# Thirty-two single zeros written into the output at the head, and the seventh pair's store cut in halves

## The chip, the cores and the metric

The kernel runs on one core of one Trainium2 chip. The metric is the device time in microseconds of one execution; the median of three runs is given. Traces come from one profiled execution, whose span runs from the first to the last instruction.

## The reference

A 3x3 convolution with padding 1 over 16 images of 64 channels and 64x64 points, to 128 output channels, in float32:

```python
x:      (16, 64, 64, 64) float32
weight: (128, 64, 3, 3) float32
x_pad = np.pad(x, ((0, 0), (0, 0), (1, 1), (1, 1)), mode='constant')
for b, co, ci, kh, kw:
    output[b, co] += weight[co, ci, kh, kw] * x_pad[b, ci, kh:kh+64, kw:kw+64]
```

The input has 16.8 MB and the output 33.6 MB.

## The kernel before

The images are worked on in eight pairs (`NP` = 8). The 64 channels of the first image of a pair lie in partitions 0 to 63, those of the second in 64 to 127, and TensorE multiplies each half by itself (`p0 = 64 * b2`).

The rows of an output image are taken two at a time. For an output row pair, the three vertical taps G0, G1, G2 are shared out: `U` is G1 times the sum of the two middle input rows (tile `ss`), `A` is (G2 - G1) and G0 on single rows, `Bt` is (G0 - G1) and G2 on single rows. The even output row is `A + U` and the odd one `Bt + U`, so 5 products of rows stand in for 6. `group` (L123) issues the matmuls of one such sum for 8 row pairs, three horizontal taps and both images, with float16 operands and float32 sums in PSUM.

At the head SyncE's queue issues the weights (`w_raw`, L42), the first pair `x0` (L45) and the pairs 1 to 3 (`xf`, L49), all in float32. VectorE sets `zeros` (L51). GpSimd casts the weights (L61); TensorE turns them (L93); ScalarE copies them to `Wt` (L94); GpSimd makes the two differences (L96, L97). Ten matmuls on `zeros` (`spin`, tile `warm`, L56) fill TensorE's time until the first pair is there. Pairs 4 to 7 are loaded by GpSimd's queue, which casts them to float16 on the way (`load`, L67, tile `xs`). For the pairs 0 to 3 ScalarE casts `x0` and `xf` to `xs` (L101, L169). The row sums `ss` are made on VectorE for pair 0 and on GpSimd for the others (L76).

The main loop (L111) runs over the pairs, and in a pair over four blocks of 8 row pairs. In each block ScalarE copies `U` from PSUM to `ut` (L164), and VectorE adds it to `A` (L174) and to `Bt` (L177) into the two output tiles `ot` of the pair. The first image of a pair is stored by SyncE's queue as soon as its last rows are added; the store of the second is put on a list, `held`, and ScalarE's queue issues it in the next block after the two `ut` copies (L171), or after the loop (L184). The helper `store` (L105) issues one DMA.

A table, `parts` (L178), says after which block which rows are stored. Pairs 0 to 6 are stored whole after the fourth block: one DMA of 2 MB for each image. Pair 7 is stored in two halves of 32 rows, after the second and the fourth block: two DMAs of 1 MB for each image.

Instructions under `keep` stay in program order on their engine. Tiles come from pools: `opool` has eight buffers of 16 KB in each partition, for `x0`, `xf` and `ot` alike. The DMAs issued by SyncE and ScalarE use eight completion semaphores in turn, so a store may have to wait for the DMA that was issued eight before it. Writes to the same image of the output are ordered by a wait on the earlier one's completion.

Of the kernel before, what the change touches and what calls it, by code (L numbers as in the profile page):

```python
# [8 lines left out]
F32 = mybir.dt.float32  # L9
# [4 lines left out]
def kernel(  # L14
# [6 lines left out]
    nc = tc.nc  # L21
    B, CI, H, W = x.shape
    CO = weight.shape[0]
    assert H == 64 and W == 64 and CI == 64 and CO == 128 and B % 2 == 0
    NP = B // 2
    RB = 8

    keep = tc.keep_in_program_order
    x_rows = x.rearrange("b c h w -> (b c) h w")
    out_rows = out.rearrange("b co h w -> b co h w")  # L30
    w_flat = weight.rearrange("co ci kh kw -> co (ci kh kw)")

    const = ctx.enter_context(tc.tile_pool(name="const", bufs=1))
# [15 lines left out]
        nc.sync.dma_start(xf[p], x_rows[128 * p : 128 * p + 128, :, :])  # L49
    zeros = const.tile([128, 512], F16)  # L50
    keep(nc.vector.memset(zeros, 0.0))  # L51
    warm = psum.tile([128, 512], F32, tag="acc", name="warm")

    def spin(n):
# [10 lines left out]
    def load(p):  # L65
        xs[p] = xpool.tile([128, H, W], F16, tag="xs", name="xs")
        keep(nc.gpsimd.dma_start(xs[p], x_rows[128 * p : 128 * p + 128, :, :]))  # L67
# [3 lines left out]
    def sums(eng, p, src, lo, n):  # L71
        if p not in ss:
            ss[p] = spool.tile([128, H // 2, W], F16, tag="ss", name="ss")
        v = src.rearrange("p (j i) c -> p j i c", i=2)
        keep(
            eng.tensor_add(  # L76
                ss[p][:, lo : lo + n, :], v[:, lo : lo + n, 0, :], v[:, lo : lo + n, 1, :]
            )
        )
# [25 lines left out]
    def store(eng, p, b2, ot, lo, hi):  # L105
        return eng.dma_start(
            out_rows[2 * p + b2, :, lo:hi, :],
            ot.rearrange("p j i c -> p (j i) c")[:, lo:hi, :],
        )

    for p in range(NP):  # L111
        if p + 1 < NP:
            for lo in (0, 16):
                sums(nc.gpsimd, p + 1, xf.get(p + 1, xs[p + 1]), lo, 16)
        if p > 0 and p + 4 < NP:
            load(p + 4)
        ots = [
            opool.tile([128, H // 2, 2, W], F32, tag="ot", name="ot") for _ in range(2)
        ]
        for blk in range(4):  # L120
            j0 = blk * RB

            def group(wi_rows):  # L123

                tiles = [
                    psum.tile([128, RB, W], F32, tag="acc", name="acc") for _ in range(2)
                ]
                n = 3 * len(wi_rows)
                i = 0
                for wi, off in wi_rows:  # L130
                    for kw in (1, 0, 2):
                        c_lo, c_hi = max(0, 1 - kw), min(W, W + 1 - kw)
                        for b2 in range(2):
                            p0 = 64 * b2
                            lo, hi = j0, j0 + RB
                            if off is None:
                                rhs = ss[p][p0 : p0 + 64, lo:hi, c_lo + kw - 1 : c_hi + kw - 1]
                            else:
                                while 2 * lo + off < 0:
                                    lo += 1  # L140
                                while 2 * (hi - 1) + off > H - 1:
                                    hi -= 1
                                first = 2 * lo + off
                                last = 2 * (hi - 1) + off
                                rhs = xs[p][
                                    p0 : p0 + 64,
                                    first : last + 1 : 2,
                                    c_lo + kw - 1 : c_hi + kw - 1,
                                ]
                            nc.tensor.matmul(  # L150
                                tiles[b2][:, lo - j0 : hi - j0, c_lo:c_hi],
                                Wt[p0 : p0 + 64, wi, kw, :],
                                rhs,
                                start=i == 0,
                                stop=i == n - 1,
                            )
                        i += 1
                return tiles

            U = group([(G1, None)])  # L160
            us = []
            for b2 in range(2):
                ut = upool.tile([128, RB, W], F32, tag="ut", name="ut")
                keep(nc.scalar.copy(ut, U[b2]))  # L164
                us.append(ut)
            if p + 1 in xf:
                q = p + 1
                for lo in {2: (0, 16), 3: (32, 48)}.get(blk, ()):
                    keep(nc.scalar.copy(xs[q][:, lo : lo + 16, :], xf[q][:, lo : lo + 16, :]))  # L169
            while held:  # L170
                keep(store(nc.scalar, *held.pop(0)))  # L171
            A = group([(G21, 1), (G0, -1)])
            for b2 in range(2):
                nc.vector.tensor_add(ots[b2][:, j0 : j0 + RB, 0, :], A[b2], us[b2])  # L174
            Bt = group([(G01, 0), (G2, 2)])
            for b2 in range(2):
                nc.vector.tensor_add(ots[b2][:, j0 : j0 + RB, 1, :], Bt[b2], us[b2])  # L177
            parts = {3: (0, 64)} if p < NP - 1 else {1: (0, 32), 3: (32, 64)}  # L178
            if blk in parts:
                lo, hi = parts[blk]  # L180
                store(nc.sync, p, 0, ots[0], lo, hi)
                held.append((p, 1, ots[1], lo, hi))
# [32 lines left out]
```

## Time and profile before

| | |
|---|---|
| Median of three runs | 126.49 us (126.47 to 126.51) |
| Profiled execution, span from first to last instruction | 124.78 us |
| Rest of an execution (median less the span) | 1.71 us |
| TensorE busy with the convolution (L150) | 9.9 to 112.5 us |
| Last store issued, landed | 113.95 us, 123.82 us |
| Bytes moved by DMA | 46.57 MB, mean 373 GB/s |
| Read from HBM, written to HBM | 17.07 MB, 33.55 MB |
| Store of 2 MB, issue to landing (median of seven, SyncE and ScalarE) | 22.0 and 18.9 us |
| Store of 1 MB, issue to landing (median of two) | 10.6 and 11.0 us |
| Granted TensorE clock over the span | 0.963 |

The time of the profiled execution itself is not listed beside its span; its span and the median are compared instead. The page counts the bytes of a DMA where they land, so that a load which turns float32 into float16 shows half of what it reads. The stage tables give, for a stretch of the span, each engine's busy time with its number of instructions, and in the last three columns the granted clock, the busy share of the 16 DMA engines and the GB/s. A packet is put to the stretch in which it starts, so a share can be a little over 1.

### The profile page before, as it was taken

To read this page: it belongs to the slowest core of one execution; us is meant where nothing else is said; L and a number is where in the kernel's file an instruction comes from. 1 tells how busy PE (TensorE), PEld (TensorE's weight loads), DVE (VectorE), ACT (ScalarE), POOL (GpSimd) and SP (SyncE) were. 2 spreads that over 40 slices of the span, in tenths; PEclk is the share of its full clock that TensorE was granted. 3 is DMA by queue.
4 is the path that set the end of the run, shared out by engine and by line. 5 is a ranking of instruction groups with operands and counts; after the bars stand their busy time and mean duration, and the time that the engine had idled before them with its cause. 6 is when DMAs were issued, how large, how long until landed. Compare 5 with 4: busy or idle time off the path is not lost.

```text
span 124.8 us, 2437 instructions
## 1 busy us (share of the span) xinstructions
PE 108.2 (87%) x988; PEld 49.3 (40%) x988; DVE 82.8 (66%) x133; ACT 52.0 (42%) x84; POOL 36.2 (29%) x27
## 2 busy tenths in 40 slices
PE   0699999999999999999999999999999999990000
PEld 0433444444444444444444444444444444440000
DVE  0016787878878787877777778777877787685000
ACT  4319749833993399333333333333333333330000
POOL 2360086294799202920067000940000000000000
PEclk9999999999999999999999999999999999999555
DMA  6899999999999999999999999999999999999991
GB/s 173 362 436 407 297 323 349 425 315 415 397 349 368 305 376 373 360 334 362 381 347 360 334 344 412 431 431 425 425 441 420 436 415 425 436 412 418 436 402 74
DMA packets 3898, 46.57 MB, mean 373 GB/s; under 512 B 432, under 2 KB 432, under 8 KB 560
## 3 DMA queue, kind: packets, MB, share of 16 engines
q1 hardware_dynamic: 2016, 25.46, 49.5%
q10 hardware_dynamic: 1296, 16.78, 31.6%
q0 software_dynamic: 576, 4.19, 16.1%
q8 instruction: 7, 0.11, 0.3%
q14 instruction: 3, 0.02, 0.0%
HBM read 17.07 MB, written 33.55 MB: 406 GB/s over the span
## 4 chain that ended last, share of the span: by engine, by line
PE 86%; DMA 2%; DVE 1%; issue 1%; POOL 1%; DVEq 0%
PE acc L150 81%; PE warm L56 4%; DMA w_raw<-in_weight_dram 2%; PE wp L93 1%; DVE ot L174 1%; POOL w L61 1%; DVE ot L177 0%; DVEq L210 0%; DVEq L174 0%
## 5 line engine op out<-in xcount | busy, mean ns | idle before, releaser
L150 PE MATMUL acc<-xs,Wt 64*128 64x504 f16 (+3 forms) x768 | 87.0, 373 | 0.0
L150 PEld LDWEIGHTS <-Wt 64*128 64x128 f16 x960 | 46.8, 94 | 56.2 <-issue 0.8
L164 ACT COPY ut<-acc 128x512 f32<-128x512 f32 x64 | 34.3, 588 | 52.9 <-issue 32.1
L174 DVE TENSOR_TENSOR ot<-acc,ut 128x512 f32<-128x512 f32 x64 | 41.2, 686 | 22.6 <-PE acc L150 18.3
L177 DVE TENSOR_TENSOR ot<-acc,ut 128x512 f32<-128x512 f32 x64 | 41.1, 684 | 0.0
L150 PE MATMUL acc<-ss,Wt 64*128 64x504 f16 (+1 forms) x192 | 26.0, 377 | 0.0
L76 POOL TENSOR_TENSOR ss<-xs 128x1024 f16<-128x1024 f16 x8 | 16.8, 2124 | 20.2 <-DMA xs<-in_x_dram 20.2
L76 POOL TENSOR_TENSOR ss<-xf 128x1024 f16<-128x1024 f32 x6 | 14.1, 2361 | 13.6 <-DMA xf<-in_x_dram 13.6
L169 ACT CAST xs<-xf 128x1024 f16<-128x1024 f32 x12 | 12.0, 1058 | 0.0
L76 DVE TENSOR_TENSOR ss<-x 128x512 f16<-128x512 f32 x4 | 2.5, 687 | 7.7 <-DMA x<-in_x_dram 7.7
L93 PE MATMUL wp<-ident,w 128*64 128x128 f16 x18 | 1.3, 328 | 4.3 <-POOL w L61 4.3
L101 ACT CAST xs<-x 128x1024 f16<-128x1024 f32 (+2 forms) x4 | 3.9, 1042 | 2.6 <-DMA x<-in_x_dram 2.6
L67 POOL DMA_DIRECT2D xs<-in_x_dram x4 | 2.4, 600 | 7.8 <-ACT xs L169 7.8
L56 PE MATMUL warm<-zeros 128*128 128x512 f16 x10 | 4.4, 631 | 0.0
L93 PEld LDWEIGHTS <-w 128*64 128x64 f16 x18 | 1.1, 210 | 4.3 <-POOL w L61 4.3
L94 ACT CAST Wt<-wp 128x384 f16<-128x384 f32 x3 | 1.2, 487 | 2.9 <-PE wp L93 2.9
L56 PEld LDWEIGHTS <-zeros 128*128 128x128 f16 x10 | 1.3, 143 | 2.3 <-issue 2.2
L94 ACT ACT_TABLE_LOAD x1 | 1.3, 1283 | 0.7 <-PEq L199 0.7
L96 POOL TENSOR_TENSOR Wt<-Wt 128x384 f16<-128x384 f16 x1 | 0.9, 907 | 1.7 <-ACT Wt L94 1.7
L61 POOL CAST w<-w_raw 128x576 f16<-128x576 f32 x1 | 0.7, 663 | 2.3 <-DMA w_raw<-in_weight_dram 2.3
L97 POOL TENSOR_TENSOR Wt<-Wt 128x384 f16<-128x384 f16 x1 | 0.9, 910 | 0.0
L51 DVE MEMSET zeros<- 128x256 uint32 x1 | 0.3, 272 | 0.9 <-PEq L199 0.9
(6 smaller groups left out, 0.9 us busy)
## 6 DMA issues: line engine op xcount, KB each, us to landing
out_dram<-ot SPq DMA_DIRECT2D x7, 2048.0 KB, 22.0
out_dram<-ot ACTq DMA_DIRECT2D x7, 2048.0 KB, 18.9
xf<-in_x_dram SPq DMA_DIRECT2D x3, 2048.0 KB, 22.1
xs<-in_x_dram POOLq DMA_DIRECT2D x4, 1024.0 KB, 23.4
x<-in_x_dram SPq DMA_DIRECT2D x1, 2048.0 KB, 7.6
out_dram<-ot SPq DMA_DIRECT2D x2, 1024.0 KB, 10.6
out_dram<-ot ACTq DMA_DIRECT2D x2, 1024.0 KB, 11.0
w_raw<-in_weight_dram SPq DMA_DIRECT2D x1, 288.0 KB, 2.8
```

The costliest lines, as they stand in the source:

```text
L56: keep(nc.tensor.matmul(warm, zeros[:, 0:128], zeros))
L61: keep(nc.gpsimd.tensor_copy(w16, w_raw))
L67: keep(nc.gpsimd.dma_start(xs[p], x_rows[128 * p : 128 * p + 128, :, :]))
L76: eng.tensor_add(ss[p][:, lo : lo + n, :], v[:, lo : lo + n, 0, :], v[:, lo : lo + n, 1, :])
L93: keep(nc.tensor.matmul(wp[q : q + 64, k * CO : k * CO + CO], w16[:, t::9], ident))
L94: keep(nc.scalar.copy(wrow(g), wp[:, 0 : 3 * CO]))
L101: keep(nc.scalar.copy(xs[0][:, lo:hi, :], x0[:, lo:hi, :]))
L150: nc.tensor.matmul(tiles[b2][:, lo - j0 : hi - j0, c_lo:c_hi], Wt[p0 : p0 + 64, wi, kw, :], rhs, start=i == 0, stop=i == n - 1,)
L164: keep(nc.scalar.copy(ut, U[b2]))
L169: keep(nc.scalar.copy(xs[q][:, lo : lo + 16, :], xf[q][:, lo : lo + 16, :]))
L174: nc.vector.tensor_add(ots[b2][:, j0 : j0 + RB, 0, :], A[b2], us[b2])
L177: nc.vector.tensor_add(ots[b2][:, j0 : j0 + RB, 1, :], Bt[b2], us[b2])
```

## The change

ScalarE first copies 32 zeros of type float32 into a tile of one element in each of 32 partitions, and its queue issues one DMA that writes them into the output: into the first point of every eighth channel of images 0 and 1. The first stores of these images write over them later, and wait for this DMA. The table `parts` now has the seventh pair (p = 6) stored in halves of 32 rows as well, like the eighth.

```diff
     zeros = const.tile([128, 512], F16)
     keep(nc.vector.memset(zeros, 0.0))
+    first = const.tile([32, 1], F32)
+    keep(nc.scalar.copy(first, zeros[0:32, 0:1]))
+    keep(
+        nc.scalar.dma_start(
+            out_rows[0:2, 0:CO:8, 0, 0:1].rearrange("b c w -> c b w"), first
+        )
+    )
     warm = psum.tile([128, 512], F32, tag="acc", name="warm")
...
-            parts = {3: (0, 64)} if p < NP - 1 else {1: (0, 32), 3: (32, 64)}
+            parts = {3: (0, 64)} if p < NP - 2 else {1: (0, 32), 3: (32, 64)}
```

In the changed program the order of the instructions on TensorE, VectorE and GpSimd is the same; ScalarE has the copy and the DMA between its table load and the first `Wt` cast, and ScalarE and SyncE each issue two stores of 1 MB for pair 6 in place of one of 2 MB.

## The prediction

> **What bounds the kernel now.** I read the page first (spans, slices, queues), then the stage table of engine and DMA time in short stretches, then the timeline around the first stores, then the packet records of the trace.
>
> ```profile
> span 124.8 us, 2437 instructions
> PE 108.2 (87%) x988; PEld 49.3 (40%) x988; DVE 82.8 (66%) x133; ACT 52.0 (42%) x84; POOL 36.2 (29%) x27
> ...
> DMA  6899999999999999999999999999999999999991
> ...
> q1 hardware_dynamic: 2016, 25.46, 49.5%
> q10 hardware_dynamic: 1296, 16.78, 31.6%
> q0 software_dynamic: 576, 4.19, 16.1%
> ```
>
> q1 is SP's queue, q10 ScalarE's, q0 GpSimd's; together their packets fill 97.2% of 16 engines' span. TensorE is busy without a break from 9.9 to 112.5 us, and the chain of waits runs through it, but the last store is issued at 113.95 us and lands at 123.82 us. The stage table says what fills those ten microseconds.
>
> ```profile
> 114.00:116.00 2.00, 0.00 (x0) 0.00 (x0) 0.00 (x0) 0.00 (x0) 0.00 (x0) 0.92 1.02 434
> 120.00:121.00 1.00, 0.00 (x0) 0.00 (x0) 0.00 (x0) 0.00 (x0) 0.00 (x0) 0.50 1.04 442
> 121.00:122.00 1.00, 0.00 (x0) 0.00 (x0) 0.00 (x0) 0.00 (x0) 0.00 (x0) 0.50 0.72 303
> 122.00:123.00 1.00, 0.00 (x0) 0.00 (x0) 0.00 (x0) 0.00 (x0) 0.00 (x0) 0.50 0.30 123
> ```
>
> The last three columns are granted clock, DMA share and GB/s. With every compute engine idle, the DMA engines still run full at about 430 GB/s until 121.2 us and then fall dry one by one. In the packet records there are 16 packets in flight from about 2 to 121.2 us. So the end is set by the sum of DMA work, about 9 us of which is still queued when TensorE stops. An earlier issue alone buys nothing; fewer engine-microseconds per packet do. The question is where the DMA engines are full but slow, and there is one place after the head:
>
> ```profile
> 24.00:25.00 1.00, 1.00 (x12) 0.49 (x10) 0.40 (x2) 0.70 (x2) 0.70 (x1) 1.00 1.01 426
> 25.00:26.00 1.00, 1.00 (x12) 0.49 (x10) 1.00 (x2) 0.00 (x0) 1.00 (x1) 1.00 1.25 459
> 26.00:27.00 1.00, 1.00 (x14) 0.41 (x10) 1.00 (x3) 0.20 (x1) 1.00 (x2) 1.00 1.17 279
> 27.00:28.00 1.00, 1.00 (x12) 0.47 (x10) 0.39 (x1) 0.87 (x2) 1.00 (x1) 1.00 0.71 213
> 28.00:29.00 1.00, 1.00 (x14) 0.47 (x10) 0.89 (x2) 0.00 (x0) 1.00 (x2) 1.00 0.77 328
> 29.00:30.00 1.00, 1.00 (x12) 0.42 (x10) 1.00 (x3) 0.00 (x0) 0.50 (x1) 1.00 1.03 442
> ```
>
> From 25 to 30 us the five rows carry 1721 KB where 5 x 430 = 2150 would go: 429 KB, or 1.0 us of all 16 engines, is lost. The packets say the same: reads of `xf` (16 KB, else 611 ns) take 800 to 1736 ns there, 0.94 us too long per engine, on all engines. The first two stores into the output were issued just before:
>
> ```profile
> 23.70 0.35 SPq L106 DMA_DIRECT2D out_dram<-ot  x1
> 24.30 0.38 ACTq L106 DMA_DIRECT2D out_dram<-ot  x1
> ```
>
> Their first packets start at 28.5 us and take 611 ns, nothing more. No later pair of stores shows such a dip (425 to 430 GB/s from 101 us on, where the seventh pair is issued). So something that happens once, with the first writes to the output, slows the reads beside it. The head has a smaller one of the same kind:
>
> ```profile
> 3.00:4.00 1.00, 0.00 (x0) 0.00 (x0) 0.00 (x0) 0.00 (x0) 0.41 (x1) 1.00 0.70 248
> 4.00:5.00 1.00, 0.69 (x12) 0.70 (x14) 0.00 (x0) 0.04 (x1) 0.25 (x1) 1.00 0.88 377
> 5.00:6.00 1.00, 1.00 (x14) 0.61 (x11) 0.00 (x0) 1.00 (x3) 0.09 (x1) 1.00 0.99 426
> ```
>
> There the first reads of the weights lose 0.26 us per engine (2304-byte packets, 93 ns as a rule, up to 498 ns at first) and the first reads of `x0` 0.41 us (up to 1506 ns).
>
> The sums below are made against the profiled execution: span 124.78 us from first to last instruction. The median of the runs is 126.49 us, so 1.71 us lies around the span; I take it as unchanged and add each difference to the median. One part in 500, 0.25 us, is about what a measurement of this kernel tells from no change.
>
> **The change, part by part.**
>
> *The zeros.* ScalarE's table load (0.74 to 2.02 us) stays first; the 32x1 copy waits for the memset (ends at 1.13 us), so it runs at about 2.05 us, and the DMA is issued at about 2.3 us. Issues on SP took 0.38 to 0.73 us, so ScalarE is free by about 3.1 us; what is queued behind it, the first `Wt` cast, starts at 4.96 us, when TensorE releases it. Cover 1.9 us, cost zero; if the cover were gone, ten `warm` matmuls (4.4 us) still stand between the casts and the first convolution matmul. The first stores of pair 0 now also wait for the zeros to land. These were issued 21 us before; the longest landing of a DMA issued at the head while others were ahead of it is 29.08 us, but that one was fourth in line on SP's queue, and ScalarE's queue is empty then. Behind that wait would stand ScalarE's `ut` copies, but I cost it at nothing.
>
> What the zeros cost the DMA engines: two packets of 4 bytes each, plus a semaphore packet. The trace has 4-byte packets only as semaphore writes (9 ns), so the floor is 3 x 9 = 27 ns per engine. The ceiling is the whole stall paid in the new place: 0.94 us. The nearest row for a small transfer that touches a new tensor is the weights' 0.26 us. I take that.
>
> What they save: if the stall at 25 to 28 us is paid for a first contact of each engine with the output, the big stores no longer pay it: 0.94 us. Below that, nothing.
>
> The Trainium skill (DMA: Bandwidth & Descriptors, "Specifications") speaks against such writes: under 512 bytes an engine reads, modifies and writes. With that page's HBM access latency ("Latency and other measured facts") of 0.2 us, up to 2 us under load, two zeros would hold an engine for 0.4 to 4 us by my estimate, and by that the change would lose. No row here has a small write into HBM, so the trace neither agrees nor disagrees.
>
> *The halves.* Pair 6 is stored as four DMAs of 1 MB, at about 94.1 and 100.5 us, with 8 KB packets in place of 16 KB ones. By the packets of q1 and q10, an 8 KB one takes 309 ns and a 16 KB one 611: 512 x 309 - 256 x 611 = 1792 ns, over 16 engines 0.11 us. Two more DMAs add 32 semaphore packets of 9 to 22 ns: 0.02 to 0.04 us. Sum +0.14 us. An earlier issue gains nothing while 16 packets are in flight, and at 94 to 103 us they are. The two issues more, 0.34 us each on queues that wait anyway, are hidden: ScalarE is idle some 2 us before each `ut` pair. The stores reuse eight completion semaphores in turn, so each waits for the DMA eight issues back; with three DMAs more the last SP store waits for that of pair 5, landed at 103.77 us, 9.6 us before it is issued at 113.35.
>
> *On the other path.* If the zeros slow `x0` by up to 1 us, TensorE starts up to 1 us later (`x0` landed at 8.78, the first convolution matmul came at 9.92 us). Some 9 us of stores are queued at the end, so this costs nothing. Nor does TensorE become the bound if the DMA saves 1 us: the last store, with 4.26 us from issue to first packet and 2.4 us for 1 MB at 430 GB/s, could end at 120.6 us, over 2 us before it would.
>
> *Sum.* -0.94 + 0.26 + 0.14 = -0.54 us; 126.49 - 0.54 = 125.95 us. With the floor for the zeros it is -0.77 us (125.7 us).
>
> **The rivals.**
>
> *The stall only moves.* The reads that were slow were those in flight beside the first writes, before any store packet ran. If a 4-byte write sets off the same thing, `x0` or `xf` is slowed by 0.94 us at 3 to 12 us, and the DMA sum is the same: -0.94 + 0.94 + 0.14 = +0.14, 126.63 us. For it: the stall precedes the first store packet, so their size does not make it. Against it: it would in part fall together with the head's own loss. Chance 0.25.
>
> *The stall stays.* It may belong to the first big stores (the turn from reading alone to reading and writing), not to the address. The zeros then add 0.03 to 0.26 us: +0.17 to +0.40, 126.66 to 126.9 us. For it: reads and writes first mix there. Against it: they mix for 50 us afterwards at 430 GB/s. Chance 0.16.
>
> *Paid twice: slower.* The zeros set off a stall at the head and the big stores one of their own, because the touched elements do not cover what the stores need, or a zero holds its engine as long as the worst packet was late (1736 - 611 = 1.1 us) and does so twice. +0.94 to 2.2 + 0.14: 127.6 to 128.8 us. The second of these is where the rule on short writes quoted above would lead; its price here is from the packets. It decides from the point where a zero costs its engine more than 0.8 us net of what it saves. For it: one packet did take 1.7 us; against it: the longest losses were on 16 KB reads. Chance 0.12.
>
> *The forecast*, stall gone for a smaller price: chance 0.47. For it: the pairs after the first, which go to other images, pay nothing, so one contact is enough for the whole output tensor; and `w_raw`, a small one, paid only 0.26 us.
>
> **How the numbers follow.** The likeliest case gives 125.95 us, on its own 125.7 to 126.2. The range reaches over the moved and the remaining stall, to 126.9, and a little below the floor, 125.6; only the rival paid twice and odd cases lie outside. Faster by over 0.2%: nearly all of the forecast, 0.46. Within 0.2% (126.24 to 126.74): most of the moved stall and a third of the one that stays, 0.26. Slower: the rest of these and the one paid twice, 0.28.
>
> **What would show it.** In the profile after: a row without a dip between 24 and 30 us (about 430 GB/s in each) shows the stall gone from there; a new dip between 3 and 13 us, on `x0` or `xf`, of more than the 0.26 us shows it moved. ScalarE's `Wt` casts should still start near 5 us. The drain should keep its shape and end about 0.5 us earlier in the span, at near 122.8 us for the last packet. 8 KB packets of pair 6 near 309 ns show the halves' price. I am wrong if the dip stays at 25 to 28 us, or if it is gone and the end does not move; then the loss was not a sum over the engines.

## The result, and the profile after

The changed kernel takes 127.34 us (median of 20 runs), the kernel before 126.50 us beside it. The ratio is 1.0058, with a 95% interval of 1.0042 to 1.0074: by it the kernel is 0.73 us slower. The medians are of all 20 runs, while the ratio leaves out one slow run of each kernel (129.94 and 129.77 us). In the profiled execution the span is 125.16 us, 0.38 us more than before. The forecast was 125.95 us, with 126.9 us as the upper end of the range.

The page's span and its queue rows (packets, MB, share of 16 engines' span):

```profile
span 125.2 us, 2444 instructions
...
q1 hardware_dynamic: 2160, 25.46, 49.1%
q10 hardware_dynamic: 1488, 16.78, 31.7%
q0 software_dynamic: 576, 4.19, 16.0%
```

The shares are those of before, within half a point. Together they are 121.2 us per engine (96.8% of 125.16 us), where before they were 121.3 us (97.2% of 124.78): the DMA work has hardly changed, and a rival by which it became dearer has nothing to stand on. The stage table at the place of the dip:

```profile
24.00:25.00 1.00, 1.00 (x13) 0.53 (x11) 0.39 (x2) 0.67 (x2) 0.55 (x1) 1.00 0.99 426
25.00:26.00 1.00, 1.00 (x12) 0.56 (x10) 1.00 (x2) 0.00 (x0) 1.00 (x1) 1.00 1.08 459
26.00:27.00 1.00, 1.00 (x14) 0.53 (x10) 1.00 (x3) 0.23 (x1) 1.00 (x2) 1.00 1.16 344
27.00:28.00 1.00, 1.00 (x12) 0.51 (x10) 0.36 (x1) 0.85 (x2) 1.00 (x1) 1.00 0.78 229
28.00:29.00 1.00, 1.00 (x12) 0.57 (x10) 0.92 (x2) 0.00 (x0) 1.00 (x1) 1.00 0.98 410
```

The dip is still there (344 and 229 GB/s). By the packets it costs 0.63 us per engine against 0.94 before; the experiments show that it varies that much by itself. The zeros run at 6.2 to 8.4 us, 4 us after their issue. The timeline has the issue, the stage table what goes on beside them:

```profile
2.25 0.66 ACTq L55 DMA_DIRECT2D out_dram<-first  x1
```

```profile
6.00:7.00 1.00, 1.00 (x4) 0.43 (x3) 0.00 (x0) 0.27 (x1) 1.00 (x2) 1.00 1.00 426
7.00:8.00 1.00, 1.00 (x4) 0.33 (x3) 0.00 (x0) 0.00 (x0) 1.00 (x2) 1.00 0.93 393
8.00:9.00 1.00, 1.00 (x5) 0.35 (x3) 0.00 (x0) 0.00 (x0) 0.39 (x1) 1.00 1.01 426
```

The 48 packets of 4 bytes (32 zeros, 16 semaphore writes) take 9 ns each as recorded, and the reads beside them are late by 0.02 us per engine. The drain:

```profile
120.00:121.00 1.00, 0.00 (x0) 0.00 (x0) 0.00 (x0) 0.00 (x0) 0.00 (x0) 0.50 1.01 426
121.00:122.00 1.00, 0.00 (x0) 0.00 (x0) 0.00 (x0) 0.00 (x0) 0.00 (x0) 0.50 0.66 279
122.00:123.00 1.00, 0.00 (x0) 0.00 (x0) 0.00 (x0) 0.00 (x0) 0.00 (x0) 0.50 0.32 131
```

The last data packet ends at 123.24 us (before 123.35) and the last store lands at 123.89 us (before 123.82). So 0.31 of the 0.38 us come after the last byte is there. The view of one line's instructions shows it, here the program's end on SyncE's sequencer (L210 before, L217 after); the two times are the starts of the first and of the last. First before, then after:

```profile
L210 SPq EVENT_SEMAPHORE  x9: 17/28/28, 113.7 to 124.7; - x9
L210 SPq DRAIN  x3: 7/7/7, 124.0 to 124.3; - x3
```

```profile
L217 SPq EVENT_SEMAPHORE  x9: 17/28/28, 123.9 to 125.1; - x9
L217 SPq DRAIN  x3: 7/7/7, 124.3 to 124.7; - x3
```

SyncE ends the program by waiting for the completion semaphores one after the other, in the order of their numbers. Seven instructions wait for the eight semaphores; the first of them waits for the first two. Before, it went through most of the list while the stores were still landing: the first of these instructions stands at 113.7 us. After, the very first one waits for the last store, and the others come behind it. The instruction records of the trace give the starts from the last landing on:

```
before: landing 123.82 | waits at 123.84 123.90                                     | drain 123.97
after:  landing 123.89 | waits at 123.91 123.98 124.04 124.10 124.16 124.22 124.28 | drain 124.35
```

Each wait takes 0.06 us even where its semaphore is long there: 0.46 us from landing to drain, against 0.14 us. The waits of SyncE's queue tell the same (waited for, us in total, times, longest): five waits before, one of 10.2 us after.

```profile
SPq L210 <- DMA out_dram<-ot: 9.9, 5, 3.6
```

```profile
SPq L217 <- DMA out_dram<-ot: 10.2, 1, 10.2
```

Why the order changed: the DMAs of SyncE and ScalarE use eight completion semaphores in turn. There were 23 of them, so the last store had the seventh; now there are 26, and it has the second. (One is the zeros', two come from the halves.) The rest of the 0.73 us is not in this profile, whose span is among the shortest of this kernel's runs (125.1 us and up); the experiments look for it.

### The profile page after: what moved, and what is told of

It reads as the page before. It is cut to its first block, busy times and chain, and to the rows that moved or that the text cites. A ratio compares the mean times of both kernels' runs of the same rounds, so it can differ in the third digit from the quotient of the medians.

```text
span 125.2 us, 2444 instructions
## 1 busy us (share of the span) xinstructions
PE 108.0 (86%) x988; PEld 56.8 (45%) x988; DVE 82.7 (66%) x133; ACT 52.1 (42%) x85; POOL 36.3 (29%) x27
## 4 chain that ended last, share of the span: by engine, by line
PE 81%; DMA 6%; DVE 2%; issue 1%; DVEq 0%; SPq 0%
PE acc L157 81%; DMA x<-in_x_dram 6%; DVE ot L181 1%; DVE ss L83 1%; DVEq L217 0%; DVE ot L184 0%; SPq L42 0%; DVEq L181 0%
## 5 line engine op out<-in xcount | busy, mean ns | idle before, releaser
L157 PE MATMUL acc<-xs,Wt 64*128 64x504 f16 (+3 forms) x768 | 93.1, 373 | 0.0
L157 PEld LDWEIGHTS <-Wt 64*128 64x128 f16 x960 | 54.4, 94 | 49.0 <-issue 1.2
L157 PE MATMUL acc<-ss,Wt 64*128 64x504 f16 (+1 forms) x192 | 31.8, 377 | 0.4 <-DVE ss L83 0.4
L63 PE MATMUL warm<-zeros 128*128 128x512 f16 x10 | 3.8, 550 | 0.0
```

What stands on the lines that cost most here:

```text
L63: keep(nc.tensor.matmul(warm, zeros[:, 0:128], zeros))
L157: nc.tensor.matmul(tiles[b2][:, lo - j0 : hi - j0, c_lo:c_hi], Wt[p0 : p0 + 64, wi, kw, :], rhs, start=i == 0, stop=i == n - 1,)
```

## The experiments

Theory: the loss is made of the waits at the end (0.32 us by count) and of the halves; the zeros cost nothing, and the dip has nothing to do with the first contact with the output. Rivals: the zeros cost time; the DMA work is dearer as a whole.

| Kernel | Waits left after the last store lands | Ratio to before (95%) |
|---|---|---|
| before | 2 | 1 |
| changed kernel | 7 | 1.0058 (1.0042 to 1.0074) |
| changed kernel, again | 7 | 1.0061 (1.0037 to 1.0085) |
| zeros alone | 1 | 1.0010 (0.9986 to 1.0034) |
| zeros alone, again | 1 | 0.9990 (0.9973 to 1.0008) |
| three DMAs of zeros, no halves | 7 | 1.0039 (1.0013 to 1.0065) |
| changed kernel, halves late | 7 | 1.0043 (1.0017 to 1.0070) |
| halves alone | 2, but 6 behind ScalarE's last store | 1.0039 (1.0024 to 1.0054) |
| halves alone, late | 6 | 1.0029 (1.0001 to 1.0057) |

The waits are counted in each kernel's own profile. The ratios of the other kernels stand in the text.

**The two parts alone, and the semaphores turned.** The first two kernels leave out one part of the change each. The next two add DMAs of 16 elements that only count the semaphores on, six to the changed kernel (shown) and three to the kernel before (`p in (0, 1, 2)`):

```diff
+    pad = const.tile([16, 8], F32)
...
+        if p in (0, 1, 2, 3, 4, 5):
+            nc.sync.dma_start(pad[:, p : p + 1], ots[0][0:16, H // 2 - 1, 1, 0:1])
```

> The zeros are written at the head, pair 6 is stored whole. 24 DMAs by SyncE and ScalarE, so the last store (ScalarE, pair 7) uses the eighth completion semaphore, the last in the list of waits at the end of the program. Theory of the end waits (the slowdown is the order in which SyncE goes through the completion semaphores at the end, 0.06 us for each wait that is left after the last landing): at most one wait is left after the last landing, against two before, so -0.06 us from the end; with the smaller dip at 26 to 29 us seen in the changed kernel (301 KB lost, 437 KB before) -0.3 us more: ratio about 0.997. Rival, the zeros cost time (their stall is added): +0.4 to +0.7 us, ratio 1.003 to 1.006.

> Pair 6 is stored in halves, no zeros. 25 DMAs: the last store of ScalarE uses the first completion semaphore, that of SyncE the eighth. Theory of the end waits: six or seven waits of 0.06 us are left after the last landing, +0.3 us if ScalarE's store lands last, and the 8 KB packets cost +0.14 us: +0.45 us, ratio 1.0035. Rival, the zeros are to blame for the slowdown: only the 0.14 us of the halves, ratio 1.001.

> The changed kernel with six DMAs of 16 elements (SBUF to SBUF, out of the finished output tile, SyncE's queue, after the first store of pairs 0 to 5) that do nothing but turn the eight completion semaphores on by six: the last store now uses the eighth. Theory of the end waits: the 0.32 us at the end go away, so 0.3 to 0.4 us faster than the changed kernel, ratio to before 1.002 to 1.003; in its profile the last landing is followed by one wait at most before the drain. Rival, the time is lost in the DMA work: as the changed kernel, ratio 1.006, or a little more for the six DMAs.

> The kernel before with three such DMAs of 16 elements (pairs 0 to 2): the semaphores stand at the end as in the changed kernel, with no zeros and no halves. Theory of the end waits: +0.3 us, ratio 1.0025, and seven waits after the last landing in the profile. Rival, the end waits do not matter: ratio 1.000 to 1.0005.

Zeros alone: 1.0010 (0.9986 to 1.0034). The 0.997 that was expected from a smaller dip did not come, and in this profile the dip costs 0.87 us per engine. Halves alone: 1.0039 (1.0024 to 1.0054). The changed kernel turned by six: 1.0022 (1.0002 to 1.0041), two waits left, 0.14 us from landing to drain. The kernel before turned by three: 1.0044 (1.0022 to 1.0066), seven waits left, 0.46 us from landing to drain, the same as in the changed kernel, with neither zeros nor halves in it:

```profile
L213 SPq EVENT_SEMAPHORE  x9: 17/28/28, 123.9 to 125.0; - x9
L213 SPq DRAIN  x3: 7/7/7, 124.3 to 124.6; - x3
```

So seven waits come with a loss where there are neither zeros nor halves, and with two waits left the changed kernel loses less (1.0022 against 1.0058). The 1.0044 is 0.56 us, more than the 0.32 us counted, which lies just within the interval.

The halves alone lose at the end too, although only two waits stand behind the store that lands last. ScalarE's store, on the first semaphore, landed at 123.78 us, SyncE's, on the eighth, at 124.08 us. The first wait of the list lasted until ScalarE's landing (the 10338 ns below); the other six then went by at 0.06 us each without a pause, and the one for SyncE's store came at 124.15 us and found it landed. The drain stands at 124.22 us, 0.44 us after ScalarE's landing and 0.25 us later than before:

```profile
L210 SPq EVENT_SEMAPHORE  x9: 17/28/10338, 113.5 to 125.0; - x9
L210 SPq DRAIN  x3: 7/7/7, 124.2 to 124.5; - x3
```

**Does the turning cost?** Halves alone turned by six, and the kernel before turned by eight, that is all the way round.

> Pair 6 in halves, no zeros, and six DMAs of 16 elements that turn the completion semaphores so that the last two stores use the same two as before (two waits left after the last landing). If the halves cost only their packets (8 KB in place of 16 KB), +0.14 us: ratio 1.001. If the halves are dearer than that (1.0039 was measured without the turn), ratio stays at 1.003 to 1.004.

> The kernel before with eight DMAs of 16 elements: the semaphores stand at the end exactly as before. It prices these DMAs themselves: 16 packets and 16 semaphore packets each, ratio 1.000 to 1.001 if they are free as supposed. If they are what made the kernel with three of them 0.5 us slower, ratio 1.005 or more, and the theory of the end waits falls.

Halves turned: 1.0042 (1.0019 to 1.0064), with three waits left in its profile (0.20 us from landing to drain) and not the two that were meant. The control failed: 1.0185 (1.0117 to 1.0253), from two runs of six. Its waits of SyncE's queue say why (L107 is the stores, not the end); the profiled run took 132.81 us, longer than those two (128.12 and 129.89), so their waits can be shorter:

```profile
SPq L107 <- DMA out_dram<-ot: 8.5, 1, 8.5
...
SPq L107 <- DMA pad<-ot: 5.6, 2, 5.0
```

Eight small DMAs more in the loop bring the DMA that last used a semaphore nearer: stores waited 8.5 and 5.0 us for it, the last one was issued at 121.58 us in place of 113.95, and the DMA queues ran dry. With six of them the small DMAs themselves still wait (3.0 to 5.3 us in all, in the kernels turned by six), so those ratios contain a price that I can't give. With three there is one wait, of 0.9 us. One such DMA was run too:

```diff
+        if p in (0,):
```

> The kernel before with one DMA of 16 elements after pair 0, so that the last store uses the eighth semaphore: one wait after the last landing. Theory of the end waits: -0.06 us and a little for the DMA, ratio 0.9995 to 1.000. If the small DMAs cost what the kernel with three of them lost (1.0044), a third of it: ratio 1.0015.

1.0020 (0.9998 to 1.0041): undecided between the two, although the median span of its runs is not longer (124.7 us beside 124.8). A cleaner way to count on was needed.

**The count changed by zeros.** Since one DMA of zeros costs nothing that can be measured (second run of the same kernel below), three of them, taken as free as well, bring the count to 26 without halves:

```diff
-            out_rows[0:2, 0:CO:8, 0, 0:1].rearrange("b c w -> c b w"), first
+            out_rows[0:2, 0:CO:8, 0, k : k + 1].rearrange("b c w -> c b w"), first     # k = 0, 1, 2
```

> The zeros alone, a second time. With one wait left at the end and no effect on the dip: ratio 0.9995 to 1.0005. If the zeros cost time by themselves, 1.001 to 1.003.

> The kernel before with three DMAs of single zeros at the head instead of one (first three points of the same channels), pair 6 whole: 26 DMAs, the semaphores at the end as in the changed kernel. Theory of the end waits: seven waits after the last landing, +0.3 us, ratio 1.002 to 1.003. Rival, the order of the waits does not matter: as with one such DMA, ratio 0.999 to 1.000.

> The changed kernel again, for the same chip: ratio 1.004 to 1.007. What it loses beyond the kernel with three DMAs of zeros is the price of the early halves: +0.14 us (0.0011) if only the packets count, up to 0.4 us (0.003) if the early issue costs too.

Zeros alone again: 0.9990 (0.9973 to 1.0008). Three DMAs of zeros: 1.0039 (1.0013 to 1.0065), seven waits left. The changed kernel beside it: 1.0061 (1.0037 to 1.0085). The median spans of the compared runs on that chip are 124.7 us before, 125.05 with three DMAs of zeros, 125.35 changed: 0.35 us for the waits, where 0.32 were counted, and 0.3 us more with the halves. The end of the kernel with three DMAs of zeros:

```profile
L218 SPq EVENT_SEMAPHORE  x9: 17/28/28, 124.4 to 125.6; - x9
L218 SPq DRAIN  x3: 7/7/7, 124.8 to 125.1; - x3
```

**The halves, issued late.** Both halves after the fourth block, so that the packets and the count stay and only the early issue goes:

```diff
+                for lo, hi in [(0, 32), (32, 64)] if p == NP - 2 else [(lo, hi)]:
+                    store(nc.sync, p, 0, ots[0], lo, hi)
+                    held.append((p, 1, ots[1], lo, hi))
```

> Pair 6 in halves, but both halves issued after the fourth block, at the time of the whole store; no zeros, 25 DMAs as in the kernel that has the halves alone (ratio 1.0039). If the halves cost by their packets and by the two DMAs more, the ratio stays at 1.003 to 1.004. If they cost by being issued early (another order of the two queues in the drain), it falls to 1.000 to 1.0015.

> Pair 6 in halves, both issued late, six small DMAs to turn the semaphores as before (two waits after the last landing). If the late halves lost only by the end waits (1.0029), nothing is left but the packets: ratio 1.000 to 1.001, against 1.0042 of the early halves with the same six DMAs; then it is the early issue that costs. If the halves cost in themselves, ratio 1.003 to 1.004.

> The changed kernel with both halves of pair 6 issued late, after the fourth block: same 26 DMAs, same seven waits, same packets. If the early issue of the halves costs, it is 0.15 to 0.3 us faster than the changed kernel, ratio 1.0025 to 1.004; if it does not, the same ratio as the changed kernel.

Late halves alone: 1.0029 (1.0001 to 1.0057) with six waits left, 0.44 us from landing to drain against 0.14 before: 0.30 us, or 0.0024, of its loss. Its last landing (123.78 us) and its drain (124.22 us) are those of the early halves alone. Turned by six: 1.0028 (1.0005 to 1.0052); here the six small DMAs and their waits are in it, and the expected 1.000 to 1.001 was missed. The changed kernel with late halves: 1.0043 (1.0017 to 1.0070), a little over the 1.0025 to 1.004 expected for a price of the early issue. Its median span is 125.1 us, 0.25 us less than with early halves and within 0.05 us of the kernel with three DMAs of zeros and no halves.

That the early issue is what costs is not shown. The intervals overlap, and so do the single spans (125.1 to 125.9 us early, 124.8 to 126.9 late). The other two pairs, which ran on different chips, differ less: halves alone 125.2 us early and 125.05 late, turned 125.1 and 125.05, with one wait more in the early one. The landing times do not settle it either: the last store lands at 123.89 to 124.31 us in the five profiles with early halves and at 123.78 to 123.91 in the three with late ones, but the three kernels with zeros and no halves gave 124.28, 123.70 and 124.38 us. What the halves cost in all lies between 0.05 and 0.3 us: 0.3 from the changed kernel against three DMAs of zeros, 0.05 from its late form, and for the halves alone 0.10 early (0.40 us longer in the median span than before, less the 0.30 us at the end) and 0.05 late.

**What the dip belongs to.** Four kernels, each the kernel before with one edit: a larger touch at the head, 1 KB in each of 128 channels of both images; pair 0 stored in halves, so that the first stores come earlier; both first stores on ScalarE's queue; both on SyncE's. The edits, cut:

```diff
+            out_rows[0:2, :, 0:4, :].rearrange("b c h w -> c b (h w)"),     # large touch
+            first.rearrange("p (b x) -> p b x", b=2),
...
-            parts = {3: (0, 64)} if p < NP - 1 else {1: (0, 32), 3: (32, 64)}
+            parts = {3: (0, 64)} if 0 < p < NP - 1 else {1: (0, 32), 3: (32, 64)}
...
+                if p == 0:
+                    held.append((p, 0, ots[0], lo, hi))     # or, for SyncE: store(nc.sync, p, 1, ots[1], lo, hi)
```

> In place of 32 single zeros ScalarE's queue writes 1 KB of zeros into every one of the 128 channels of images 0 and 1 at the head (256 KB), pair 6 whole. If the dip at 25 to 29 us is paid for a first contact with the addresses, it is gone from there (430 GB/s in every row) and another one stands where these writes run. If it belongs to the first large stores themselves, it stays at 25 to 29 us with 0.6 to 1.0 us lost. Time: 256 KB more at 430 GB/s, +0.6 us, ratio 1.005, less 0.9 us if the dip goes.

> The kernel before with pair 0 stored in halves: the first stores are issued at about 17 us instead of 23.7 us. If the dip follows the first stores, it stands at 18 to 22 us; if it belongs to that place in the reads (or to that time), it stays at 25 to 29 us. Time about as the kernel before, +0.1 us for 8 KB packets, up to +0.3 us for the end waits (25 DMAs).

> Both stores of pair 0 are issued by ScalarE's queue, none by SyncE's, whose queue still holds the loads of pair 3. If the dip comes from stores standing behind loads in SyncE's queue, it goes: the rows at 24 to 30 us show 430 GB/s and the time falls by 0.6 to 0.9 us, ratio 0.993 to 0.995. If it comes with the first large stores by whatever queue, it stays and the time is that of the kernel before, ratio 1.000.

> Both stores of pair 0 are issued by SyncE's queue behind the loads, none by ScalarE's, so no second queue begins beside the reads of pair 3. If the dip comes from ScalarE's queue starting its stores beside SyncE's loads, it goes, ratio 0.993 to 0.995. If it comes with the first large stores by whatever queue, it stays, ratio 1.000.

Stage table of the kernel with the large touch, then of the one with pair 0 in halves:

```profile
26.00:27.00 1.00, 1.00 (x13) 0.86 (x11) 1.00 (x3) 0.19 (x1) 1.00 (x1) 1.00 1.08 410
27.00:28.00 1.00, 1.00 (x13) 0.86 (x10) 0.40 (x1) 0.89 (x2) 1.00 (x2) 1.00 1.14 279
28.00:29.00 1.00, 1.00 (x13) 0.89 (x10) 0.88 (x2) 0.00 (x0) 1.00 (x1) 1.00 0.77 311
```

```profile
21.00:22.00 1.00, 1.00 (x13) 0.81 (x10) 0.28 (x2) 1.00 (x3) 0.00 (x0) 1.00 0.89 238
22.00:23.00 1.00, 1.00 (x14) 0.89 (x11) 1.00 (x3) 1.00 (x2) 0.00 (x0) 1.00 0.81 303
...
26.00:27.00 1.00, 1.00 (x13) 0.80 (x10) 1.00 (x3) 0.26 (x1) 1.00 (x1) 1.00 1.03 442
27.00:28.00 1.00, 1.00 (x12) 0.81 (x10) 0.33 (x1) 0.82 (x2) 1.00 (x1) 1.00 0.98 418
```

With 256 KB written over all channels of both images between 5.6 and 16.7 us, the dip stands where it stood; with the first stores issued six microseconds earlier, it stands earlier, and 26 to 28 us are full. So it belongs to the first large stores; by what they slow the reads was not found. Issued by ScalarE alone it stays (0.88 us per engine, ratio 1.0020, 0.9989 to 1.0050), by SyncE alone too (0.87 us; 1.0050, 1.0014 to 1.0087), so no single queue makes it. The large touch took 1.0034 (1.0004 to 1.0063), the early first pair 1.0077 (1.0049 to 1.0105), more than the +0.4 us expected at most: six waits are left, and by the packet records the engines stand idle for 1.3 us each between 100 and 105 us. Why both stores on SyncE's queue lose 1.0050, where 1.000 was expected, was not traced.

**One more try at the count.** The load of pair 3 in four DMAs of 32 partitions:

```diff
+        n = 32 if p == 3 else 128
+        for q in range(0, 128, n):
+            nc.sync.dma_start(xf[p][q : q + n], x_rows[128 * p + q : 128 * p + q + n, :, :])
```

> The kernel before with the load of pair 3 cut in four DMAs of 32 partitions each (same rows of 16 KB): 26 DMAs by SyncE and ScalarE, as in the changed kernel, and nothing else changed. Theory of the end waits: seven waits after the last landing in place of two, +0.3 us, ratio 1.0025. Rival, the order of the end waits does not matter: ratio 1.000 to 1.0005.

1.0344 (1.0300 to 1.0387): neither. The load itself became slow:

```profile
23.00:24.00 1.00, 1.00 (x13) 0.87 (x10) 1.00 (x2) 0.80 (x2) 0.00 (x0) 1.00 1.22 262
24.00:25.00 1.00, 1.00 (x13) 0.92 (x11) 0.40 (x2) 0.62 (x2) 0.00 (x0) 1.00 1.21 246
25.00:26.00 1.00, 1.00 (x12) 0.88 (x10) 1.00 (x2) 0.00 (x0) 0.53 (x1) 1.00 0.89 180
26.00:27.00 1.00, 1.00 (x13) 0.86 (x10) 1.00 (x3) 0.28 (x1) 1.00 (x1) 1.00 0.72 147
```

About half the rate of a load over 128 partitions, for 8 us. It tells nothing of the waits.

No version beat the kernel before by more than the measurement tells: the zeros alone, with one wait left, come nearest (0.9990, 0.9973 to 1.0008).

## Why the prediction was wrong

*What bounds the kernel: right in the main.* The DMA engines drain at about 430 GB/s until 121 us, and nothing on TensorE's side moved the end. But the sum over the 16 engines does not fix the end to some tenths of a microsecond, since the engines run dry one by one and the last of them counts. In the second profile of the changed kernel the dip cost 0.36 us per engine less than before (0.58 against 0.94), and still the last data packet ended 0.49 us later (123.84 against 123.35).

*What the zeros save, -0.94 us: the step that failed first.* It took the dip for a first contact with the addresses. The dip follows the first large stores wherever they are issued and is not lessened by writes to the same images. Its 0.94 us is one draw: profiles without any touch at the head show 0.52 to 1.03 us per engine, profiles with one 0.58 to 0.90. The rival that the stall stays was the true one, with a chance of 0.16; its argument, that it may belong to the first big stores, is what the early first pair shows. Its time, 126.66 to 126.9 us, was too short as well, since it had no waits at the end.

*What the zeros cost, +0.26 us: mis-sized.* Measured as 0.02 us per engine beside them and 0.9990 in time. The Trainium skill's rule on writes under 512 bytes (DMA: Bandwidth & Descriptors, "Specifications"), from which, with that page's access latency, I estimated 0.4 to 4 us per engine, is not borne out here as a price: the engines' other packets were late by 0.02 us. The wait of the first stores for the zeros was rightly put at nothing: the zeros landed at 8.8 us, 15 us before these stores. (The load with the landing of 29.08 us was the fifth on SyncE's queue, not the fourth; nothing hangs on it.)

*The halves, +0.14 us: neither confirmed nor refuted.* The packets were priced rightly (309 and 611 ns in the changed kernel too). The comparisons give 0.05 to 0.3 us for the halves in all. That the early issue is free was concluded from 16 packets always in flight; this shows that it can't gain, not that it can't lose, and whether it loses stays open.

*The three DMAs more, costed at nothing: the step that missed the largest term of the loss.* I followed the eight semaphores in turn for the waits before a store, where there is slack (9.0 us in the changed kernel's profile, where 9.6 was said), and not to the end of the program, where the same turn decides how many waits of 0.06 us stand behind the last landing: 0.32 us.

With nothing for the zeros' saving and their cost, +0.32 for the waits and +0.05 to +0.3 for the halves the sum is +0.37 to +0.62 us. The median spans of the last comparison differ by 0.65 us (124.7 and 125.35); the ratio of the times gives 0.73 us, with an interval of 0.53 to 0.94. The 0.3 us is read from the same spans, so the agreement at the upper end proves nothing: some 0.3 us of the loss, beyond the waits, has no cause that the runs show, only the halves as its likeliest place.

## What to carry to other kernels

When the end of a kernel is a DMA landing, read what the queue that ends the program still has to do after it: which semaphore the last transfer holds and how many waits stand behind it. Here every DMA that SyncE or ScalarE issued more or less turned that order, so a change that only adds a small transfer can cost or gain some tenths of a microsecond (0.08 to 0.46 us from landing to drain) for a reason that is not in the transfer. A dip in bandwidth that comes once is not yet a cost of addresses; move the transfers that seem to cause it before building a remedy.

## What the runs showed of the hardware

A wait of SyncE for a semaphore that has long been reached takes 0.06 us, so a list of seven costs 0.46 us with the step to the drain, and a list of one 0.08 us (zeros alone). The first large stores slow the reads beside them by 0.5 to 1.0 us per engine once. It begins before they write: in the kernel before, their first packets start at 28.5 us, when the dip ends; with pair 0 in halves they start at 22.0 us, with reads of 700 to 1190 ns since 20.2 us. Thirty-two writes of 4 bytes into HBM cost nothing measurable (0.02 us per engine, ratio 0.9990). A load cut in four DMAs of 32 partitions ran at 147 to 262 GB/s, where one over 128 partitions gives about 430. A DMA on an empty queue began about 4 us after its issue under load (the zeros: 2.25 to 6.25 us), and 1.0 us on the idle chip (the weights: 0.74 to 1.75 us).
